# Band copies of a macaron block's FFNs on ScalarE or GpSimd

## The chip, the cores and the metric

One core of a Trainium2 chip runs the whole block. A core has five engines with a queue each, worked off in order: TensorE (PE: matmuls; PEld: its loads of weights), VectorE (DVE), ScalarE (ACT), GpSimd (POOL) and SyncE (SP, which here only issues DMAs). DMAs can also be issued from ACT's and POOL's queues. The metric is the device time of one execution in microseconds (us), as the median of several runs; lower is better.

## The reference

One layer: a gated FFN added with weight 0.5, a mixer of a short convolution and gated linear attention, a second FFN, a last norm; all in float32 on 512 rows of width 1024, hidden width 2816.

```python
def swiglu(x, w_gu, w_down):
    g, u = jnp.split(x @ w_gu, 2, axis=-1)
    return (jax.nn.silu(g) * u) @ w_down
...
    for l in range(DEPTH):
        x = x + FFN_RES_WEIGHT * swiglu(rmsnorm(x, norm_ffn1_g[l]), ffn1_w_gu[l], ffn1_w_down[l])
        x = x + hybrid_mixer(rmsnorm(x, norm_mix_g[l]), w_in[l], conv_w[l], gate_w_up[l], gate_b[l],
                             gla_norm_g[l], w_out_conv[l], w_out_gla[l], w_o[l])
        x = x + FFN_RES_WEIGHT * swiglu(rmsnorm(x, norm_ffn2_g[l]), ffn2_w_gu[l], ffn2_w_down[l])
    return rmsnorm(x, final_norm_g)
```

## The kernel before

**Products.** A float32 product is made from three matmuls in a rounded float32 type: each operand v is split into h (v cast, by ScalarE) and l = v - h (by VectorE), and h*h + h*l + l*h is summed in PSUM. For weights this is `wh` (line L386, ScalarE) and `wl` (L387, VectorE), made two steps ahead into three buffers each, from raw weights `f` that SyncE's DMAs load into ten buffers.

**Sets.** Most matrix products are cut 2 x 2 and done with seven block products instead of eight, called m1, p2, q6, p5, q7, p3 and p4 in the code. Sums of weight blocks that some of them need are made in place: by DMAs that add one `f` to another, issued from GpSimd's queue (`add`, L352), or by VectorE (L364, L394). A *tall* set turns the product round: the activations are the stationary operand and the weights the moving one of 128x512 (`Tall.run`, L712); a plain set has 128x256 (`Set.run`, L625). A tall set's seven products have two halves each, so it takes 14 steps of 12 matmuls. Some products are copied on from PSUM by ScalarE: L718 (the running sum m1), L835 and L838 (u and a kept q6), L633 (a kept q6 or q7 of a plain set).

**The hidden layer.** In an FFN's up projection, a tall set gives four of the 22 blocks of the hidden layer, but with rows and columns exchanged (tokens on partitions). The down projection needs them the other way round, in `hid`. For that VectorE turns blocks of 32 x 32 in place into `z` (L875), and then 16 copies of 32 partitions x 512 elements put each band into its place in `hid`: `move(f, a, q)` (L881) takes band a of `z`, columns of quarter q, to quarter q of `hid`'s partitions. `z` has one buffer, so the next set's turns wait for all 16 copies.

The first FFN (PLAIN1 = 4) has four tall sets (hidden blocks 4, 8, 12, 16) and then a plain one (20, 21); the copies of its last tall set are called one by one at later steps (`late_move`), down into the first steps of the down projection. The second FFN has five tall sets (0, 6, 10, 14, 18) and a plain set after the first; its last two are turned by PE (`turn`, L869), so it has 48 copies, and the first FFN 64. The other sets' 16 copies are called over the ten steps that follow the set. During the second FFN, GpSimd makes 32 copies of the same form for the residual (`natural_move`, L1060), from blocks that VectorE turns (L1054). The plain set there is turned by PE at L916.

**Order.** PE's order is as written. The other engines' order is chosen ahead of the run by a list scheduler, which knows the instructions' dependences and gives each engine one fixed queue; an instruction in `keep_in_program_order` stays behind everything written before it on its engine. Waits between engines are semaphores.

Of the kernel before, what the change touches and what calls it, by code (L numbers as in the profile page):

```python
# [234 lines left out]
def block_kernel(ctx: ExitStack, tc: tile.TileContext, xT, vecs, gf, gup, wgl, wts, out):  # L235
    nc = tc.nc
# [568 lines left out]
    def ffn(up, down, norm, nxt, plain, at):  # L805
# [71 lines left out]
        def move(f, a, q):  # L877

            src = zs[f][32 * a : 32 * (a + 1)].rearrange("p t (b r) -> p b t r", r=P)
            dst = hid[32 * q : 32 * (q + 1), f : f + 4].rearrange("p b (t r) -> p b t r", r=P)  # L880
            nc.scalar.copy(dst[:, :, :, 32 * a : 32 * (a + 1)], src[:, :, :, 32 * q : 32 * (q + 1)])  # L881

        def up_set(i):
            f = [f for kind, f in UPS[up] if kind == "set"][i]
# [122 lines left out]
        def late_move():  # L1007
            if late:
                move(*late.pop(0))
# [3 lines left out]
        for i, (kind, f) in enumerate(UPS[up]):  # L1013
            if kind == "set":
                if not plain:
                    at_step(begin(i + 1)[0], lambda f=f: turn_pair(f))
                continue
            quads = [(f, a, q) for a in range(4) for q in range(4)]
            if f in by_tensor:
                turns = (begin(i + 1) if i + 1 < len(UPS[up]) else  # L1020
                         [((down, 0), 1, "m1"), ((down, 0), 0, "p2")])
                for key, js in zip(turns, ((0, 1), (2, 3))):
                    at_step(key, lambda f=f, js=js: turn(f, js))
            elif f == last:
                late.extend(quads)
            else:
                after = keys[ends[f] + 1 : ends[f] + 11]
                for n, m in enumerate(quads):
                    at_step(after[n * len(after) // 16], lambda m=m: move(*m))
# [870 lines left out]
```

## Time and profile before

| | |
|---|---|
| median of 3 runs | 1156.43 us (1155.9 to 1156.73) |
| profiled execution | 1157.14 us, span of the trace 1155.4 us, granted TensorE clock 0.999 |
| busy share of the span | PE 99%, PEld 86%, DVE 77%, ACT 62%, POOL 13% |
| first FFN's up projection, tall sets | about 50 to 208 us |
| second FFN's tall sets with copies | about 820 to 980 us |

The profile is of one execution. Its groups read: line, engine, operation, tile written <- tiles read, shape, count | busy us, mean ns | idle us of the engine before them and what ended that idle time. In a timeline a row is start, length, engine, line, operation, tiles, count, and in brackets an idle time ahead of it with what ended it. Matmuls overlap, so their starts, not their lengths, give PE's pace.

### The profile page before, as it was taken

To read this page: it belongs to the slowest core of one execution; us is meant where nothing else is said; L and a number is where in the kernel's file an instruction comes from. 1 tells how busy PE (TensorE), PEld (TensorE's weight loads), DVE (VectorE), ACT (ScalarE), POOL (GpSimd) and SP (SyncE) were. 2 spreads that over 40 slices of the span, in tenths; PEclk is the share of its full clock that TensorE was granted. 3 is DMA by queue.
4 is the path that set the end of the run, shared out by engine and by line. 5 is a ranking of instruction groups with operands and counts; after the bars stand their busy time and mean duration, and the time that the engine had idled before them with its cause. 6 is when DMAs were issued, how large, how long until landed. Compare 5 with 4: busy or idle time off the path is not lost.

```text
span 1155.4 us, 16314 instructions
## 1 busy us (share of the span) xinstructions
PE 1144.6 (99%) x6284; PEld 996.3 (86%) x6284; DVE 893.9 (77%) x1061; ACT 714.7 (62%) x923; POOL 149.5 (13%) x191
## 2 busy tenths in 40 slices
PE   9999999999999999999999999999999999999997
PEld 7888888889988888889999998888888878888886
DVE  7976776798887975767797999555786666889966
ACT  6568778755452757565665567534668588675543
POOL 0011111001021111101011110000111344110100
PEclk9999999999999999999999999999999999999999
DMA  9587786657674386778576787934485977787711
GB/s 363 112 205 161 180 220 157 173 143 175 174 220 136 82 228 163 188 217 227 137 173 147 198 205 182 322 115 128 97 207 147 235 181 167 180 223 176 179 40 73
DMA packets 60381, 203.20 MB, mean 176 GB/s; under 512 B 6960, under 2 KB 7088, under 8 KB 60304
## 3 DMA queue, kind: packets, MB, share of 16 engines
q0 software_dynamic: 19648, 71.31, 33.6%
q1 hardware_dynamic: 38064, 126.14, 32.2%
q10 hardware_dynamic: 2592, 4.72, 1.1%
q8 instruction: 49, 0.80, 0.3%
q14 instruction: 28, 0.23, 0.1%
HBM read 124.55 MB, written 8.39 MB: 115 GB/s over the span
## 4 chain that ended last, share of the span: by engine, by line
PE 90%; ACT 6%; DVE 2%; issue 1%; ACTq 0%; POOL 0%; POOLq 0%
PE mm L712 42%; PE mm L625 24%; PE mm L443 6%; PE mm L421 3%; PE mm L419 3%; PE mm L420 3%; ACT wh L386 3%; ACT hid L881 2%; PE mm L461 1%; PE mm L460 1%; PE mm L462 1%; DVE wl L387 1%; PE mm L1161 1%; PE mm L1160 1%; PE mm L1162 1%
## 5 line engine op out<-in xcount | busy, mean ns | idle before, releaser
L387 DVE TENSOR_TENSOR wl<-f,wh 128x1024 fp32r<-128x1024 f32 (+1 forms) x349 | 424.5, 1221 | 173.2 <-ACT wh L386 168.2
L386 ACT CAST wh<-f 128x1024 fp32r<-128x1024 f32 (+1 forms) x349 | 364.3, 1048 | 297.5 <-PE mm L712 94.8
L712 PE MATMUL mm<-wh,op 128*128 128x512 f32 x1680 | 522.9, 390 | 0.0
L712 PEld LDWEIGHTS mm<-wh,op 128*128 128x128 f32 x1680 | 315.4, 188 | 65.2
L712 PE MATMUL mm<-wl,op 128*128 128x512 f32 x840 | 327.7, 390 | 1.9 <-DVE wl L387 1.8
L625 PE MATMUL mm<-op,wh 128*128 128x256 f32 x1456 | 263.4, 283 | 1.3 <-ACT tp L633 1.3
L352 POOL DMA_DIRECT2D f<-f x132 | 113.8, 865 | 895.6 <-DVE wl L387 459.1
L625 PEld LDWEIGHTS mm<-op,wh 128*128 128x128 f32 x1456 | 227.4, 192 | 2.3 <-ACT tp L633 1.5
L625 PE MATMUL mm<-op,wl 128*128 128x256 f32 x728 | 206.1, 283 | 0.1
L712 PEld LDWEIGHTS mm<-wl,op 128*128 128x128 f32 x840 | 157.7, 188 | 36.9 <-DVE wl L387 4.7
L625 PEld LDWEIGHTS mm<-op,wl 128*128 128x128 f32 x728 | 139.4, 191 | 0.3 <-DVE wl L387 0.3
L881 ACT COPY hid<-z 32x512 f32<-32x512 f32 x112 | 69.3, 618 | 5.6 <-DVE z L875 3.9
L683 ACT CAST op<-hid 128x1024 fp32r<-128x1024 f32 x42 | 44.0, 1050 | 19.6 <-PE mm L712 14.1
L684 DVE TENSOR_TENSOR op<-hid,op 128x1024 fp32r<-128x1024 f32 x42 | 51.3, 1223 | 5.2 <-ACT op L683 4.8
L421 PE MATMUL mm<-op,wl 128*128 128x512 f32 x132 | 51.5, 390 | 0.0
L420 PE MATMUL mm<-op,wh 128*128 128x512 f32 x132 | 51.4, 389 | 0.0
L419 PE MATMUL mm<-op,wh 128*128 128x512 f32 x132 | 51.4, 389 | 0.0
L443 PE MATMUL mm<-op,wh 128*128 128x512 f32 x192 | 49.0, 397 | 0.0
L443 PEld LDWEIGHTS mm<-op,wh 128*128 128x128 f32 x192 | 36.4, 192 | 8.1 <-ACT wh L386 0.4
L394 DVE TENSOR_TENSOR f<-f,f 128x1024 f32<-128x1024 f32 x26 | 31.8, 1234 | 7.1 <-issue 4.3
L421 PEld LDWEIGHTS mm<-op,wl 128*128 128x128 f32 x132 | 24.8, 188 | 5.4 <-DVE wl L387 0.3
L420 PEld LDWEIGHTS mm<-op,wh 128*128 128x128 f32 x132 | 24.8, 188 | 5.1
(331 smaller groups left out, 1197.7 us busy)
## 6 DMA issues: line engine op xcount, KB each, us to landing
f<-wts SPq DMA_DIRECT2D x219, 512.0 KB, 4.5
f<-f POOLq DMA_DIRECT2D x132, 512.0 KB, 5.2
xs<-X POOLq DMA_DIRECT2D x8, 256.0 KB, 4.1
ga<-tp ACTq DMA_DIRECT2D x8, 256.0 KB, 4.8
gb<-tp ACTq DMA_DIRECT2D x8, 256.0 KB, 5.5
tp<-ga SPq DMA_DIRECT2D x8, 256.0 KB, 6.1
tp<-gb SPq DMA_DIRECT2D x8, 256.0 KB, 5.1
X<-xs SPq DMA_DIRECT2D x8, 256.0 KB, 6.5
```

Of the source, the lines that this page charges most:

```text
L352: nc.gpsimd.dma_start(out_, a, accum_op=ALU.add)
L386: nc.scalar.copy(h[:, :w], raw[:, :w])
L387: nc.vector.tensor_tensor(out=l[:, :w], in0=raw[:, :w], in1=h[:, :w].bitcast(F32), op=ALU.subtract)
L419: nc.tensor.matmul(o, wh, ah, start=first, stop=False)
L420: nc.tensor.matmul(o, wh, al, start=False, stop=False)
L421: nc.tensor.matmul(o, wl, ah, start=False, stop=last)
L443: nc.tensor.matmul(o[c], w[:, s : s + P], a[k], start=k == 0 and j == 0, stop=k == kt - 1 and j == 2)
L625: nc.tensor.matmul(to, ww[:, s], aa[:, t], start=fresh and k == 0 and e == 0 and j == 0, stop=k == 3 and j == 2, skip_group_check=True)
L683: nc.scalar.copy(hv, v)
L684: nc.vector.tensor_tensor(out=lv, in0=v, in1=hv.bitcast(F32), op=ALU.subtract)
L712: nc.tensor.matmul(self.bank[b][e], aa[:, c], ww, start=fresh and i == 0 and n == 0, stop=k == 3 and n == 2, skip_group_check=True)
L881: nc.scalar.copy(dst[:, :, :, 32 * a : 32 * (a + 1)], src[:, :, :, 32 * q : 32 * (q + 1)])
```

## The change

In `move`, a copy whose quarter q is 1 or 3 (first FFN) or 3 (second FFN) is made by GpSimd (now at line L883) instead of ScalarE (now L885), and stays in program order there. That is 8 of the 16 copies of each of four sets in the first FFN (32), and 4 of the 16 of each of three sets in the second (12); 68 stay on ScalarE.

```diff
-            nc.scalar.copy(dst[:, :, :, 32 * a : 32 * (a + 1)], src[:, :, :, 32 * q : 32 * (q + 1)])
+            dst, src = dst[:, :, :, 32 * a : 32 * (a + 1)], src[:, :, :, 32 * q : 32 * (q + 1)]
+            if q in ((1, 3) if plain else (3,)):
+                tc.keep_in_program_order(nc.gpsimd.tensor_copy(dst, src))
+            else:
+                nc.scalar.copy(dst, src)
```

The scheduler then orders ScalarE's queue anew. Names below are the tile written and the tiles read, with their numbers. On ScalarE, in the second half of the copies of the first FFN's first tall set (z131):

```order
 L386 CAST wh152_923<-f116_706 128x1024
-L881 COPY hid20_190<-z131_794 32x16x32 x2
 L386 CAST wh154_940<-f126_753 128x1024
-L881 COPY hid20_190<-z131_794 32x16x32 x2
 L838 COPY tp156_956<-mm136_834 128x512
-L881 COPY hid20_190<-z131_794 32x16x32
 L838 COPY tp157_958<-mm137_835 128x512
 L386 CAST wh158_962<-f114_702 128x1024
-L881 COPY hid20_190<-z131_794 32x16x32 x2
 L386 CAST wh160_980<-f124_749 128x1024
-L881 COPY hid20_190<-z131_794 32x16x32
```

Ahead of wh152 stand eight copies before and eight now; ahead of wh158 and wh160 thirteen and fifteen before, and eight now. The second and third set (z180, z229) have the same pattern.

At the end of the first FFN's up projection, with the copies of its fourth tall set (z279): first ScalarE (L1067 and L683 cast operands of the down projection from `hid`, L633 empties the bank of a kept q7), then GpSimd.

```order
 L386 CAST wh295_1828<-f247_1484 128x1024
-L881 COPY hid20_190<-z279_1717 32x16x32 x3
-L1067 CAST op321_1977<-hid20_190 128x1024
+L1071 CAST op321_1977<-hid20_190 128x1024
+L885 COPY hid20_190<-z279_1717 32x16x32
+L683 CAST op325_2010<-hid20_190 128x1024
 L633 COPY tp297_1856<-mm271_1648 128x512
```

Two copies fewer and one cast more (op325) stand between wh295 and the copy out of the bank.

```order
 L352 DMA f292_1822<-f291_1820 128x1024
+L883 COPY hid20_190<-z279_1717 32x16x32
 L352 DMA f327_2014<-f329_2018 128x1024
+L883 COPY hid20_190<-z279_1717 32x16x32
 L352 DMA f328_2016<-f327_2014 128x1024
+L883 COPY hid20_190<-z279_1717 32x16x32
 L352 DMA f363_2278<-f364_2280 128x1024
```

Copies of the fourth set now stand behind adding DMAs in GpSimd's queue, the last behind the one into f328. The cast op382 on ScalarE, which reads blocks 16 to 19 of `hid`, now waits for GpSimd.

On ScalarE in the second FFN, towards the end of the copies of its second tall set (z1255; the third, z1304, is alike):

```order
 L838 COPY tp1280_8650<-mm1260_8520 128x512
-L881 COPY hid1105_7600<-z1255_8478 32x16x32
 L838 COPY tp1281_8652<-mm1261_8521 128x512
 L386 CAST wh1282_8658<-f1240_8388 128x1024
-L881 COPY hid1105_7600<-z1255_8478 32x16x32 x2
 L386 CAST wh1284_8678<-f1248_8432 128x1024
-L881 COPY hid1105_7600<-z1255_8478 32x16x32
```

Of this set's copies thirteen stood ahead of wh1282 before, and twelve do now; ahead of wh1284 fifteen before, and twelve now. In the first tall set of that FFN (z1178) the four copies between the casts wh1206 and wh1211 are gone from ScalarE.

## The prediction

> **What bounds the kernel now.** I read the engines' busy shares first, then the groups by line.
>
> ```profile
> PE 1144.6 (99%) x6284; PEld 996.3 (86%) x6284; DVE 893.9 (77%) x1061; ACT 714.7 (62%) x923; POOL 149.5 (13%) x191
> L387 DVE TENSOR_TENSOR wl<-f,wh 128x1024 fp32r<-128x1024 f32 (+1 forms) x349 | 424.5, 1221 | 173.2 <-ACT wh L386 168.2
> L881 ACT COPY hid<-z 32x512 f32<-32x512 f32 x112 | 69.3, 618 | 5.6 <-DVE z L875 3.9
> L1060 POOL COPY X<-hid 32x512 f32<-32x512 f32 x32 | 25.9, 808 | 3.7 <-DVE hid L1054 2.5
> ```
>
> TensorE (PE) is the bound: 1144.6 of 1155.4 us. ScalarE is idle for over a third of the span, so the 69.3 us of band copies cannot be worth 69.3 us; they are worth only the holes in PE that ScalarE's backlog makes. For those I followed the chain of waits through the first FFN, and looked where it leaves PE.
>
> ```profile
> 108.98 1.06 ACT wh L386
> 110.07 1.24 DVE wl L387
> 111.35 24.59 PE mm L712 x107
> ...
> 149.97 23.27 PE mm L712 x102
> ...
> 188.60 5.55 PE mm L712 x23
> ...
> 209.31 0.67 DVE z L875
> 209.98 1.12 DVE wl L387
> 211.14 2.90 PE mm L625 x22
> ...
> 220.49 0.59 ACT tp L633
> 221.12 6.01 PE mm L625 x48
> ```
>
> Rows are start, length, what. PE resumes at 111.35, 149.97 and 188.60 after a weight split (cast wh by ScalarE, remainder wl by VectorE), at 211.14 after VectorE's own burst of transposes, and at 221.12 after ScalarE emptied a PSUM bank. The chain says who came last, not how long PE stood still; that comes from PE's timeline, as the start of a matmul minus the start at which it was due.
>
> ```profile
> 187.76 0.61 PE L712 MATMUL mm<-wh,op 128*128 128x512 f32 x2
> 188.60 0.50 PE L712 MATMUL mm<-wl,op 128*128 128x512 f32 x1 [0.22 <-DVE wl L387]
> 188.94 0.40 PE L712 MATMUL mm<-wh,op 128*128 128x512 f32 x1
> ...
> 219.52 0.28 PE L625 MATMUL mm<-op,wl 128*128 128x256 f32 x1
> 221.12 0.50 PE L625 MATMUL mm<-op,wh 128*128 128x256 f32 x2 [1.32 <-ACT tp L633]
> ...
> 941.79 0.61 PE L712 MATMUL mm<-wh,op 128*128 128x512 f32 x2
> 943.12 0.50 PE L712 MATMUL mm<-wl,op 128*128 128x512 f32 x1 [0.72 <-DVE wl L387]
> ...
> 980.88 0.61 PE L712 MATMUL mm<-wh,op 128*128 128x512 f32 x2
> 981.95 0.50 PE L712 MATMUL mm<-wl,op 128*128 128x512 f32 x1 [0.45 <-DVE wl L387]
> ```
>
> The pitch of a 128x512 matmul is 24.59/107 = 0.23 us. After the two from 187.76 the next was due at 188.22 and came at 188.60: 0.38 late, and the one behind it started 0.34 instead of 0.23 later, so the hole is 0.49. The chain's rows at 111.35 and 149.97 begin the same kind of hole, which I take at the same 0.49. The 128x256 pitch is 6.01/48 = 0.125: 221.12 was due at 219.64, a hole of 1.48, about 1.58 with the restart. In the second FFN: due 942.25, came 943.12, 0.98 with the restart; due 981.34, came 981.95, 0.72. One more stands where PE turns tiles:
>
> ```profile
> 886.17 1.43 PE L916 MATMUL aux<-ident,tp 128*128 128x128 f32 x8
> 887.36 0.47 PE L712 MATMUL mm<-wh,op 128*128 128x512 f32 x1
> ...
> 1003.62 1.04 PE L869 MATMUL aux<-ident,z 128*128 128x128 f32 x8
> 1004.42 0.47 PE L712 MATMUL mm<-wh,op 128*128 128x512 f32 x1
> ```
>
> Eight turns take 1.19 from their start to the next matmul at 886.17 and 0.80 at 1003.62: 0.39 lost. All holes that ScalarE's copies can have a part in: 3 x 0.49 + 1.58 + 0.39 + 0.98 + 0.72 = 5.1 us, 0.45% of the kernel. That is the ceiling.
>
> **The change, part by part.** 32 copies of the first FFN and 12 of the second leave ScalarE's queue for GpSimd's: 44 x 0.62 = 27 us of ScalarE. What counts is how many of them stood ahead of each late instruction.
>
> Behind the first tall set of the first FFN (z131) five copies fewer stand ahead of wh158, which is the cast at 108.98 that PE waited for.
>
> ```profile
> 93.00:111.00 18.00, 18.00 (x81) 14.67 (x79) 9.33 (x9) 17.44 (x26) 2.58 (x3) 1.00 0.58 130
> ```
>
> In this stretch (columns: length, then busy us of PE, PEld, DVE, ACT, POOL) ScalarE is busy 17.44 of 18 us, so five copies fewer bring the cast 5 x 0.62 = 3.1 us forward, against 0.49 us needed: the hole goes, and PE itself is late next. Second and third set are ordered alike: 3 x 0.49 = **1.47 us**.
>
> At the hole at 221.12, behind the fourth set (z279), two copies go from ahead of L633, but the cast op325 of 1.05 us comes in: 2 x 0.62 - 1.05 = **0.19 us** of the 1.58. The rest of this hole stays, and so does the one at 211.14, which VectorE's burst makes. The second FFN:
>
> ```profile
> 881.15 2.50 ACT L881 COPY hid<-z 32x512 f32<-32x512 f32 x4
> ...
> 939.38 0.62 ACT L881 COPY hid<-z 32x512 f32<-32x512 f32 x1
> ...
> 940.50 1.05 ACT L386 CAST wh<-f 128x1024 fp32r<-128x1024 f32 x1
> ...
> 941.58 1.49 DVE L387 TENSOR_TENSOR wl<-f,wh 128x1024 fp32r<-128x1024 f32 x1 [2.21 <-ACT wh L386]
> ```
>
> At 886 the four copies from 881.15 go from ahead of the activation that the turns wait for: 2.5 us against 0.39 needed, **0.39 us**. At 943 and 982 only one copy fewer stands ahead of the late cast (12 instead of 13, the one at 939.38), 0.62 us. At 943 that leaves 0.87 - 0.62 = 0.25 and a restart if the split still takes 1.49, and nothing if it takes its usual 1.22: a gain of 0.6 to 0.98, I take **0.8**. At 982 0.61 was missing and 0.62 comes: 0.4 to 0.72, I take **0.65**.
>
> What GpSimd pays. The same copy form, 32x512, stands in its row L1060 at 808 ns mean, so 44 cost 36 us on an engine that is busy 13%. Where it pushes others:
>
> ```profile
> 895.66 5.09 POOL L1060 COPY X<-hid 32x512 f32<-32x512 f32 x6
> ...
> 900.26 1.57 DVE L387 TENSOR_TENSOR wl<-f,wh 128x1024 fp32r<-128x1024 f32 x1 [1.93 <-ACT wh L386]
> ```
>
> This split began among six copies of L1060 and took 1.57 instead of the 1.22 of L387's group: a copy in progress holds VectorE up by as much as 0.35 us, and a split holds a copy up likewise (six in 5.09 us, 0.85 each, where ScalarE takes 0.62). The bounds of this term are 0 and 44 x 0.35 = 15.4 us of VectorE. From 93 to 111 VectorE works 9.33 of 18 us and waits for casts in the rest, so there I cost it at 0: its idle time covers it, and without that cover each delay would be PE's. I charge it only at 943 and 982, in the choices above, because those two splits come with no room at all. The Trainium skill, "SBUF — State Buffer", section "Who interferes with whom", says that a VectorE instruction with two SBUF inputs contends with a GpSimd instruction that reads SBUF and that the later one fully blocks; by it a delay could reach one copy's 0.61 us, not 0.35, and at 943 and 982 nothing would be gained, 1.45 us less in the sum.
>
> GpSimd's queue also holds the DMAs that add weights (L352), and copies now stand among them. The tightest place is the end of the first FFN: the last copy of z279 stands behind the adding DMA into f328, and ScalarE's operand cast op382 gains a wait for it.
>
> ```profile
> 265.95 0.86 POOL L352 DMA_DIRECT2D f<-f  x1 [4.90 <-DVE wl L387]
> ...
> 272.94 1.04 ACT L683 CAST op<-hid 128x1024 fp32r<-128x1024 f32 x1
> ```
>
> The copy can end at 265.95 + 0.86 + 0.8 = 267.6 and is needed at 272.94: 5.3 us of room, cost 0. Earlier sets have more, since z is next written a whole set later. A DMA behind copies starts at most some copies later; six copies are 6 x 0.81 = 4.9 us, and the engine idles longer than that before most of them (L352 in the stretch from 93: 2.58 busy of 18). I cost that at 0, covered by this idle time.
>
> Sum: 1.47 + 0.19 + 0.39 + 0.8 + 0.65 = **3.5 us**. The profiled execution took 1157.14 (span 1155.4, 1.7 around it), 0.7 above the median 1156.43. Taken off: 1153.6 profiled, a span near 1151.9, and 1152.9 as the median. This measurement can tell about 0.2%, 2.3 us, from no change.
>
> **Rivals.**
> 1. Everything goes: the order at 221 turns out harmless as well, all 5.1 us: 1151.4. For it, ScalarE's other copies there shrink too; against it, the cast moved ahead of L633. 0.10.
> 2. The second FFN gives nothing, because copies in progress block the two splits that have no room: 3.5 - 1.45 = 2.05, so 1154.4. For it, the 1.49 and 1.57 us rows above; against it, only four copies per set move there. Chance 0.19. (The Trainium skill's page named above makes it the rule whenever the copy starts first; the rows here show delays of part of a copy.)
> 3. PE runs ahead and meets weights that have not landed. Nine casts already wait for loads (row below: us in total, times, longest); none of these waits reaches PE now, and one that does, at its longest, takes back 1.8 of the 3.5: 1154.7. 0.06.
>
> ```profile
> ACT wh L386 <- DMA f<-wts: 14.6, 9, 1.8
> ```
>
> Two end on the other side.
>
> 4. Slower: VectorE's splits become the bound under GpSimd's copies. 44 delays of 0.35 are 15 us; with 40% of that on PE, 6.2 us against 3.5, the kernel takes 1159. It decides from a quarter (3.5 of 15.4). Against it, VectorE idles half of these stretches. 0.04.
> 5. Slower: a copy is stuck behind an adding DMA and op382 waits. It must come 5.3 us later than worked out before it costs anything, 8.8 us later to undo the gain, and 11.4 us later for 1159. 0.03.
>
> **How the numbers follow.** My forecast has 0.58. Faster by over 0.2% (below 1154.1): forecast and rival 1, 0.68. Within 0.2%: rivals 2 and 3, 0.25. Slower: rivals 4 and 5, 0.07. The range runs from rival 1 (1151.4) to rival 3 (1154.7), each widened by the 0.5 us by which the runs shown lie from their median (1155.9 against 1156.43): 1150.9 to 1155.2. That leaves out most of rivals 4 and 5 and a little on either side.
>
> **What would show it.** The row of ScalarE's copies falls to x68, GpSimd gets x44 at 0.6 to 0.9 us. In the chain, PE runs through 111, 150 and 187 without a split before it; near 219 there is still a wait for L633 of over 1 us; the turns near 885 take 0.8; near 941 and 980 the waits for wl are below 0.3. I am wrong if PE shows new waits for wl inside the sets, if a transpose into z or an operand cast waits for GpSimd, or if the hole near 219 is gone.

## The result and the profile after

The change makes the kernel faster: 1150.49 us in the median of 6 runs (1150.15 to 1150.89) against 1156.65 for the kernel before beside it (6 runs, 1155.9 to 1157.47), a ratio of 0.9947 with an interval of 0.9934 to 0.996. That is 6.2 us, where 3.5 were forecast; the time lies 0.4 under the low end of the range. The profiled execution took 1150.53 (span 1148.8), against 1157.14 (span 1155.4).

From the page of the changed kernel, the engines' busy shares and the groups that the change touches (L883 is the new copy on GpSimd, L885 ScalarE's, L1064 the residual's copy, formerly L1060):

```profile
PE 1141.2 (99%) x6284; PEld 996.6 (87%) x6284; DVE 901.0 (78%) x1061; ACT 687.8 (60%) x879; POOL 199.1 (17%) x235
L387 DVE TENSOR_TENSOR wl<-f,wh 128x1024 fp32r<-128x1024 f32 (+1 forms) x349 | 428.0, 1231 | 164.7 <-ACT wh L386 159.7
L883 POOL COPY hid<-z 32x512 f32<-32x512 f32 x44 | 45.8, 1041 | 22.1 <-DVE z L875 20.5
L885 ACT COPY hid<-z 32x512 f32<-32x512 f32 x68 | 42.0, 618 | 2.5 <-DVE z L875 1.5
L1064 POOL COPY X<-hid 32x512 f32<-32x512 f32 x32 | 29.4, 919 | 1.5 <-DVE hid L1058 0.2
```

44 copies went over. On GpSimd one takes 1041 ns in the mean, more than the 600 to 900 forecast, and VectorE is busy 7.1 us longer (901.0 against 893.9). TensorE still sets the time: the chain of waits through the first FFN, which before came back to PE from other engines at 111.35, 149.97, 188.60, 211.14 and 221.12, now stays on it (start, length, what):

```profile
85.96 105.63 PE mm L712 x466
191.58 2.87 PE mm L625 x24
194.46 10.91 PE mm L712 x48
205.36 17.27 PE mm L625 x144
```

PE's holes, measured as before (start of a matmul minus the start at which it was due, restarts included), in us:

| place in the kernel before | before | after |
|---|---|---|
| 111, 150, 188 (splits behind the tall sets) | 3 x 0.49 | 0 |
| 211 (split of a plain step) | 0.36 | 0 |
| 221 (wait for L633) | 1.58 | 0 |
| 886 (turns) | 0.39 | 0.09 |
| 943 | 0.98 | 0.30 |
| 982 | 0.72 | 0 |

Together 5.1 us less. PE runs its 6284 matmuls in one order in all kernels, so their starts can also be compared one by one. By that count the change ends 6.6 us earlier: 0.9 in the first 25 us, ahead of any tall set's copies; 3.7 between 100 and 230; 2.0 from 880 on; nothing elsewhere. So 5.7 us lie behind the copies, and the table has all but small delays beside its places (0.12 near 228, 0.13 near 893, and 0.04 to 0.06 at each of the three splits).

PE's timeline after, at the last two places where something is left: the eight turns now take 0.80 from their start to the next matmul, and one wait for a split remains.

```profile
881.56 1.03 PE L920 MATMUL aux<-ident,tp 128*128 128x128 f32 x8
882.36 0.48 PE L712 MATMUL mm<-wh,op 128*128 128x512 f32 x1
```

```profile
936.63 0.61 PE L712 MATMUL mm<-wh,op 128*128 128x512 f32 x2
937.27 0.50 PE L712 MATMUL mm<-wl,op 128*128 128x512 f32 x1
```

### The profile page after: what moved, and what is told of

The parts are those of the page before. It is cut to its first block, busy times and chain, and to the rows that moved or that the text cites. A ratio compares the mean times of both kernels' runs of the same rounds, so it can differ in the third digit from the quotient of the medians.

```text
span 1148.8 us, 16324 instructions
## 1 busy us (share of the span) xinstructions
PE 1141.2 (99%) x6284; PEld 996.6 (87%) x6284; DVE 901.0 (78%) x1061; ACT 687.8 (60%) x879; POOL 199.1 (17%) x235
## 4 chain that ended last, share of the span: by engine, by line
PE 98%; DVE 1%; ACT 1%; issue 0%; ACTq 0%; POOL 0%; POOLq 0%
PE mm L712 49%; PE mm L625 25%; PE mm L443 6%; PE mm L420 3%; PE mm L419 3%; PE mm L421 3%; PE mm L461 1%; PE mm L460 1%; PE mm L462 1%; PE mm L1166 1%; PE mm L1164 1%; PE mm L1165 1%; PE aux L1510 1%; PE aux L1513 0%; PE aux L1493 0%; PE aux L281 0%
## 5 line engine op out<-in xcount | busy, mean ns | idle before, releaser
L625 PEld LDWEIGHTS mm<-op,wh 128*128 128x128 f32 x1456 | 227.4, 192 | 0.7
L625 PEld LDWEIGHTS mm<-op,wl 128*128 128x128 f32 x728 | 139.4, 192 | 0.0
L683 ACT CAST op<-hid 128x1024 fp32r<-128x1024 f32 x42 | 44.0, 1050 | 22.5 <-PE mm L712 14.1
L883 POOL COPY hid<-z 32x512 f32<-32x512 f32 x44 | 45.8, 1041 | 22.1 <-DVE z L875 20.5
L885 ACT COPY hid<-z 32x512 f32<-32x512 f32 x68 | 42.0, 618 | 2.5 <-DVE z L875 1.5
L443 PEld LDWEIGHTS mm<-op,wh 128*128 128x128 f32 x192 | 36.2, 190 | 7.6
L394 DVE TENSOR_TENSOR f<-f,f 128x1024 f32<-128x1024 f32 x26 | 34.5, 1342 | 5.0 <-issue 3.9
L1064 POOL COPY X<-hid 32x512 f32<-32x512 f32 x32 | 29.4, 919 | 1.5 <-DVE hid L1058 0.2
```

The lines of the kernel that those rows point to most:

```text
L443: nc.tensor.matmul(o[c], w[:, s : s + P], a[k], start=k == 0 and j == 0, stop=k == kt - 1 and j == 2)
L625: nc.tensor.matmul(to, ww[:, s], aa[:, t], start=fresh and k == 0 and e == 0 and j == 0, stop=k == 3 and j == 2, skip_group_check=True)
L683: nc.scalar.copy(hv, v)
L883: tc.keep_in_program_order(nc.gpsimd.tensor_copy(dst, src))
```

## Where the holes at 211 and 221 came from

The prediction gave the hole at 221 a gain of 0.19 and the one at 211 none, and both went wholly. It put the one at 211 down to VectorE's transposes. But the chain of waits before, a few rows further up than the prediction showed it, leads from these transposes back to the cast at 205.25, and from there on to L633 as well:

```profile
205.25 1.06 ACT wh L386
206.34 1.23 DVE wl L387
207.56 1.20 DVE tp L594 x2
...
214.04 0.60 DVE z L875
215.29 0.62 ACT hid L881
```

What changed ahead of that cast is seen on VectorE, GpSimd and ScalarE. Before (rows: start, length, engine, line, operation, tiles, count, idle time ahead and what ended it by the profile):

```profile
188.58 1.23 DVE L364 TENSOR_TENSOR f<-f,f 128x1024 f32<-128x1024 f32 x1
...
190.33 0.86 POOL L352 DMA_DIRECT2D f<-f  x1 [11.25 <-ACT hid L881]
197.22 0.86 POOL L352 DMA_DIRECT2D f<-f  x1 [6.03 <-DVE wl L387]
...
205.25 1.05 ACT L386 CAST wh<-f 128x1024 fp32r<-128x1024 f32 x1 [4.39 <-PE mm L712]
...
220.49 0.58 ACT L633 COPY tp<-mm 128x512 f32<-128x512 f32 x1
```

And after:

```profile
183.84 1.22 DVE L364 TENSOR_TENSOR f<-f,f 128x1024 f32<-128x1024 f32 x1 [0.30 <-DMA f<-wts]
...
186.74 0.86 POOL L352 DMA_DIRECT2D f<-f  x1 [6.15 <-DVE wl L387]
192.95 0.86 POOL L352 DMA_DIRECT2D f<-f  x1 [5.35 <-DVE tp L840]
...
200.05 1.06 ACT L386 CAST wh<-f 128x1024 fp32r<-128x1024 f32 x1 [1.75 <-DMA f<-f]
...
215.10 0.58 ACT L633 COPY tp<-mm 128x512 f32<-128x512 f32 x1
```

The same five steps stand 3.6 to 5.4 us earlier, while PE itself is 2.6 ahead there. The third set's copies (z229) on ScalarE had made the cast at 186.23 late; behind its remainder on VectorE the sum at L364 was late; GpSimd's first adding DMA overwrites a block that this sum reads, so it waits for the sum, and the second for the first to land; and the cast of wh280 reads what the second wrote. The times of the semaphores in the traces bear out each link. Before, the sum ended at 189.80, and the first add started 0.53 later; it landed at 196.71, and the second started 0.51 later; that landed at 205.15, and the cast started 0.10 later. After, the sum ended at 185.06, and what the first add waited for was a load of weights, which landed at 186.18. So copies of one set cost PE time 35 us later, behind the next set, by way of two transfers.

The lateness at GpSimd is not all of it. Against PE, the cast came 2.6 us earlier: 1.0 is the earlier first add, and 1.6 is that the two transfers took 5.7 and 7.0 us from start to landing, where they took 6.4 and 7.9 before. In the twelve traces they take 5.4 to 7.0 and 5.6 to 8.2. What sets their time, no run shows.

The profile of before named PE as what ended the cast's idle time of 4.39 us, and I believed it; the profile of after names the transfer. (The names in the adds' rows, ACT hid and DVE wl, mislead in the same way.) The row of such a DMA does not show its landing: 0.86 us long at 192.95, while the data landed at 199.95 and the cast behind it starts at 200.05. The Trainium skill, "Perfetto Trace Analysis", section "DMA Instruction — SWDGE (GPSIMD)", says as much: the interval shown ends with the last descriptor, not with the data.

## The experiments

Each stood beside the kernel before on the same chip: 1156.38 us in the first group, 1156.52 in the second, 1156.55 in the third. Unless said otherwise, the edit is to the changed kernel's one line of condition, `if q in ((1, 3) if plain else (3,)):`, and nothing else.

**One FFN alone.**

```diff
+            if plain and q in (1, 3):
```

> Only the first FFN's 32 copies go to GpSimd. My theory: the holes near 111, 150, 187, 211 and 221 us all go (3 x 0.49 + 0.37 + 1.58 = 3.4 us against the kernel before, about 1153.2), and those near 886, 943 and 982 stay at 0.4, 1.0 and 0.7. Rival (the prediction's own account, and something else in the second FFN for the rest): 1.7 us, about 1155, with a hole of over 1 us near 219.

1153.1 us, ratio 0.9973 (0.9961 to 0.9984): 3.3 us of gain. The holes at 111, 150, 188 and 211 are gone and the second FFN's are there, but 0.5 is left of the one at 221, which the theory had go. In the first FFN the queues hold the change's order; the first add started 0.9 us earlier than there, but the two took 6.8 and 8.0 us to land instead of 5.7 and 7.0. So a part of this hole comes and goes with the time of the transfers.

```diff
+            if not plain and q == 3:
```

> Only the second FFN's copies with q == 3 go to GpSimd (12 of 48); the first FFN's all stay on ScalarE. Theory (the gain is the sum of the holes that the chain of late casts made): the holes near 886, 943 and 982 lose 0.39, 0.68 and 0.73 us as in the whole change, 1.8 us together, so 1154.6 against 1156.4; the first FFN's holes (111, 150, 188, 211, 221) stay at 0.49, 0.49, 0.49, 0.4 and 1.6. Rival (the second FFN gives more than its holes show, by what the whole change and the first FFN alone differ, 1153.1 - 1150.5 = 2.6 us): 1153.8. Second rival (of the prediction: the second FFN's turns are paced by something other than the copies): 1156.2 or more.

1154.58 us, ratio 0.9981 (0.9972 to 0.999): 1.9 us, which is the theory's 1.8. The first FFN's holes are all there. The two parts alone, 3.3 and 1.9, add up to 5.2, near the 5.1 of the table; as each is known to 1.0 to 1.3 us, that is agreement in size and no more.

**One set alone, and all but that one.** The first FFN's sets write `hid` from block f = 4, 8, 12, 16; the condition is narrowed to f == 12 (third set), f == 16 (fourth), and to all but f == 12 (no set of the second FFN starts there).

```diff
+            if plain and f == 12 and q in (1, 3):
```

> Only eight copies of the first FFN's third tall set go to GpSimd. Theory: the backlog of this set makes not only the hole at 188 but, by way of the sum f262 and the two adding DMAs into f246 and f244 behind it, the late transposes of the fourth set, and so the holes at 211 and 221: 0.49 + 0.37 + 1.58 = 2.4 us gained, about 1154.2, with holes left only near 111, 150 and in the second FFN. Rival: the hole at 221 belongs to the fourth set's own copies ahead of the bank's evacuation; then 0.5 us is gained, about 1156.1, and 211 and 221 stay.

```diff
+            if plain and f == 16 and q in (1, 3):
```

> Only eight copies of the first FFN's fourth tall set go to GpSimd. Theory: its own copies are not what makes the hole at 221; 0.2 us gained (two copies fewer, one cast more ahead of the evacuation), about 1156.4, hole still 1.3 or more. Rival: 1.6 us gained, about 1155.0, hole gone.

```diff
+            if f != 12 and q in ((1, 3) if plain else (3,)):
```

> The change without the third set: its 16 copies stay on ScalarE. Theory: the holes at 188, 211 and most of 221 come back, 0.49 + 0.37 + 1.4 = 2.3 us slower than the whole change, about 1152.8. Rival: only 0.5 us is given back, about 1151.0.

The third set alone: 1154.32 us, ratio 0.9983 (0.9974 to 0.9992), 2.1 us of gain. PE's holes at 188, 211 and 221 are gone, 111 and 150 stay. The fourth alone: 1156.38, ratio 1.0 (0.9991 to 1.0009), and all holes stay, 1.27 us at 219 and 0.58 at 211, which is 0.31 less and 0.22 more than before. So what stands between wh295 and L633, which the prediction had counted copy by copy, is worth 0.3 us at that hole and nothing that shows in the time. All but the third: 1152.28, ratio 0.9966 (0.9953 to 0.9978), 1.8 us above the change. The holes of 0.49 at 186 and of 1.12 near 217 are back; the one at 211 isn't, though the theory had it come back too. The first add starts 1.7 us behind the hole at 186 and takes 6.4 to land, both as before; the second took 7.4 instead of 7.9, about what is missing at 211 and 221. ScalarE and GpSimd there:

```profile
188.38 0.86 POOL L352 DMA_DIRECT2D f<-f  x1 [11.25 <-ACT hid L885]
195.28 0.86 POOL L352 DMA_DIRECT2D f<-f  x1 [6.04 <-DVE wl L387]
...
202.74 1.05 ACT L386 CAST wh<-f 128x1024 fp32r<-128x1024 f32 x1 [3.87 <-DMA f<-f]
...
217.67 0.58 ACT L633 COPY tp<-mm 128x512 f32<-128x512 f32 x1
```

One caution on single profiles: with the first FFN, the third or the fourth set alone, the second FFN shows 0.5 to 0.8 us more of holes than before, though its queues hold the order of before. By so much two executions can differ there.

**Without the second add.** A direct test of the link: the kernel before, ScalarE making all 112 copies, with one adding DMA left out, the one at 197.22 (the 26th of `add`; a part of the sum of weights is then missing).

```diff
-        def add(self, out_, a):
-            nc.gpsimd.dma_start(out_, a, accum_op=ALU.add)
+        def add(self, out_, a, nth=iter(range(999))):
+            if next(nth) not in (25,): nc.gpsimd.dma_start(out_, a, accum_op=ALU.add)
```

> The kernel before, with all copies on ScalarE, but without the one weight add into f244 that GpSimd issued at 197.22 us (this leaves a part of the weights' sum out of the computation). Theory (the hole at 221 follows the landing of that add at 205.15, through the cast of wh280 right behind it): the cast starts when its buffer is free, near 201 to 203, the wait for L633 near 220 shrinks from 1.58 us to under 0.3, the hole of 0.4 near 211 goes as well, and the time is 1154.4 to 1155.0 against 1156.5, though ScalarE still makes all of its copies. Rival (the reading on record: the cast is paced by PE, and the fourth set's copies on ScalarE make L633 late): the hole stays at 1.4 us or more and the time at 1156.2 or more.

1154.32 us, ratio 0.9982 (0.9974 to 0.9991): 2.2 us. Its adds, the cast, the copy out of the bank, and then the chain of waits behind the third set:

```profile
189.75 0.86 POOL L352 DMA_DIRECT2D f<-f  x1 [11.23 <-ACT hid L881]
204.51 0.86 POOL L352 DMA_DIRECT2D f<-f  x1 [13.90 <-DVE wl L387]
```

```profile
201.90 1.06 ACT L386 CAST wh<-f 128x1024 fp32r<-128x1024 f32 x1 [1.67 <-PE mm L712]
...
217.35 0.58 ACT L633 COPY tp<-mm 128x512 f32<-128x512 f32 x1
```

```profile
188.01 5.51 PE mm L712 x23
193.52 2.87 PE mm L625 x24
196.40 10.91 PE mm L712 x48
207.30 17.27 PE mm L625 x144
```

The cast now does wait for PE, 1.67 us and no more; PE runs from 188.01 through both places without a hole, while 111, 150 and 188 are as they were. The other instructions stand in the order of before on every queue. So both holes hang on this one transfer, and ScalarE's copies of the fourth set, all still there, do no harm. Put beside each other, with PE's need taken as 0.12 us behind the start of its matmul before:

| kernel | first add | second add | cast of wh280 | L633 starts | PE wants its result | hole |
|---|---|---|---|---|---|---|
| before | 190.33 | 197.22 | 205.25 | 220.49 | 219.6 | 1.58 |
| all but the third set | 188.38 | 195.28 | 202.74 | 217.67 | 217.3 | 1.12 |
| copies twice (below) | 187.30 | 194.81 | 201.89 | 216.83 | 217.1 | 0.48 |
| the change | 186.74 | 192.95 | 200.05 | 215.10 | 216.7 | 0 |
| without the second add | 189.75 | none | 201.90 | 217.35 | 218.7 | 0 |

From the cast to L633 it takes 14.9 to 15.5 us in all five, and L633 another 0.6. The hole is what remains.

**What GpSimd can bear.** All copies on GpSimd, then each of the 44 made twice.

```diff
+            if True:
```

> All 112 copies of the tall sets go to GpSimd. Theory (VectorE and GpSimd hold each other up and GpSimd's queue is in order): a copy there took 1.04 us in the mean against 0.62 on ScalarE, so a set's 16 take some 17 us of GpSimd against 10 of ScalarE before; the weight adds queue behind them and the last copies come some 5 us later than in the change, against 1.6 us that the wait for L633 near 215 has to spare. So the gain is lost again in part or whole: 1152 to 1160, with holes of 1 us and more behind every set. Rival (only what ScalarE is rid of counts, GpSimd's time is free): at or under the change, 1149.5 to 1150.5.

1154.83 us (11 runs, 1152.63 to 1156.42), ratio 0.9982 (0.9973 to 0.9991): faster than before by 1.7 and slower than the change by 4.3, so the theory's size came and the rival's didn't. But its place was wrong. In the profiled execution, the fastest of the 11, the first FFN has no holes at all, with GpSimd busy 31.7 of the 55 us from 170 to 225; the largest hole is in the second FFN. There the residual's copies use the same queue, the adds come late behind them, and four casts in a row and a sum (L394) wait for transfers (the last of them and the sum below), where in the change the casts at this place wait for PE:

```profile
958.67 4.35 POOL L883 COPY hid<-z 32x512 f32<-32x512 f32 x4
...
963.45 1.05 ACT L386 CAST wh<-f 128x1024 fp32r<-128x1024 f32 x1 [1.45 <-DMA f<-f]
...
963.43 1.32 DVE L394 TENSOR_TENSOR f<-f,f 128x1024 f32<-128x1024 f32 x1 [0.87 <-DMA f<-f]
...
965.94 0.50 PE L712 MATMUL mm<-wl,op 128*128 128x512 f32 x1 [1.71 <-DVE wl L387]
```

What makes the slower ten runs up to 3.8 us slower than this one, no trace shows.

```diff
+                for _ in range(2):
+                    tc.keep_in_program_order(nc.gpsimd.tensor_copy(dst, src))
```

> As the change, but every copy on GpSimd is made twice in a row (the same values to the same place), so that GpSimd and its lock on the memory beside VectorE are used twice as long and ScalarE's part is unchanged. Theory (the copies on GpSimd lie beside other work; VectorE has spare time of 20 per cent): a set's GpSimd part rises from 8.3 to 16.6 us (first FFN); an add may come some us later, but most lands ahead of its cast: 1150.5 to 1152. Rival (GpSimd's time is near the path, the change just fits): each set comes 3 to 8 us later than its splits are wanted, 1155 or more.

1153.2 us (1151.52 to 1154.19), ratio 0.9969 (0.9957 to 0.998): 2.7 us slower than the change, between the two expectations. Two of the places are adding DMAs again: the second add at 194.81 instead of 192.95 (0.48 us of hole, in the table), and at 251 a hole of 1.6 us. The add ahead of that one starts at 243.28, where the change has 239.10. Of these 4.2 us, 1.7 are the two copies ahead of it, which took 4.17 beside VectorE's two-input operations, where the change has one of 2.44. The other 2.4, of which PE's own lateness is 0.9, are that the add before waited so much longer for a sum of VectorE (L364), which here works without a pause from 215.83 on, with three operations stretched to 1.6 us by the doubled copies:

```profile
239.15 4.17 POOL L884 COPY hid<-z 32x512 f32<-32x512 f32 x2
243.28 0.86 POOL L352 DMA_DIRECT2D f<-f  x1
```

```profile
247.92 1.05 ACT L386 CAST wh<-f 128x1024 fp32r<-128x1024 f32 x1 [7.06 <-DMA f<-f]
```

**Half in both FFNs.**

```diff
+            if q in (1, 3):
```

> Half of the copies in both FFNs go to GpSimd (24 of 48 in the second in place of 12). Theory: what is left of ScalarE's lateness in the second FFN is the hole of 0.30 us near 937 and 0.1 near 882; with half of the copies gone the cast ahead of 937 comes 1.2 us earlier, and the time is 1150.0 to 1150.4. Rival (GpSimd's queue, which there also has the 32 copies of L1064 and the adds, is the bound): the 12 copies more cost 12 x 1.04 = 12.5 us of GpSimd over three sets, the adds come up to 4 us later and a hole of 1 us or more opens: 1151.5 to 1154.

1150.43 us (1150.24 to 1150.55), ratio 0.9946 (0.9933 to 0.9958). The 0.30 at 937 is gone, the span is 1148.2 instead of 1148.8, and the change repeated in the third group has 1150.63: a difference of 0.1 to 0.2 us, which these runs do not tell from none. No hole over 0.1 us is left at any of these places, so this is as far as moving the copies goes.

**The change again.**

> The whole change, unaltered, beside the kernel before on the chip of this call. The holes that went come to 5.3 us and the medians of the first comparison differ by 6.2. Theory (the holes are all of it): 5.3 us under the kernel before, 1151.2 at 1156.5. Rival (half a microsecond or more comes from elsewhere): 6.0 us or more under it.

1150.63 us (1150.16 to 1151.35), ratio 0.995 (0.9936 to 0.9964), 5.9 us under the kernel before. It falls between theory and rival, and the interval (4.2 to 7.4 us) holds both. The profiles say more. Matmul by matmul, this execution gains 5.6 us behind the first copies, and the one of the first comparison 5.7. The other 1.2 and 0.9 of the spans' differences lie in the first 25 us, where no edit changes the order of a queue and the profile of the kernel before is the slowest of the twelve (the others are 0.3 to 1.3 ahead of it). So that part is a difference between executions. What the medians, 6.2 and 5.9, show beyond 5.7 is well within their intervals.

## The prediction, step by step

- **Three holes of 0.49 (1.47).** Right: all three are gone, and the splits are out of the chain. That such a hole belongs to its own set is shown for the third, which alone removed just the one at 188 of the three; the first and second set were only moved together.
- **Hole at 221 (0.19), hole at 211 (0).** This is the step that failed, and that the hole near 219 is gone is the sign of being wrong that I had named. I counted the instructions between wh295 and L633, where the change does little (fourth set alone: 0.3 at this hole, 0 in the time), and took the cast at 205.25 as paced by PE because its row said so. It waited for an adding DMA, which the third set's copies had delayed. The term was worth 1.58 and 0.36 instead of 0.19, some 1.75 us, most of the 2.2 that my 3.5 lacked of the 5.7.
- **The ceiling of 5.1** was too low: the hole at 211, which I charged to VectorE's burst, belonged in it too, and 5.7 came.
- **Turns at 886 (0.39), 943 (0.8), 982 (0.65).** 0.30, 0.68 and 0.72: a sum of 1.7 against 1.84. Rival 2 (nothing from the second FFN) is out: that part alone gained 1.9. The hole left at 937 is where the lock below takes its share, as I had allowed in the choice of 0.8.
- **GpSimd's and VectorE's cost (0).** Right on PE's path, though the size was missed: 1041 ns for a copy instead of 808. VectorE's 7.1 us over 44 copies are 0.16 us for each, under half of the bound of 0.35, though a single operation was stretched by up to 0.41: 23 of the 44 copies took their usual 0.60 to 0.62. Rival 4, VectorE's splits as the bound, did not come. With twice the copies (14.1 us more on VectorE, 908.0) late adds made 2.1 of the 2.7 us lost, and VectorE's lateness had a part in one of them. Rival 5 did not come either.
- **Rival 3 (weights not landed).** The casts wait for loads less than before: 6.7 us in four waits, where 14.6 in nine stood.

```profile
ACT wh L386 <- DMA f<-wts: 6.7, 4, 1.8
```

- **Chances.** Rival 1, that everything goes, is what happened, at 0.10. I worked it out as harmless order at 221; its cause was a link that I had not looked for.

## What to carry to other kernels

A hole that stands far behind a busy engine's backlog may still be made by it: follow each late instruction through every step that it waits for, the transfers issued from another engine's queue above all, until the chain reaches work that is early, and do not stop at the engine which the row names. Count a queue's relief by the deadline it feeds and not by its busy time: 27 us taken off ScalarE gave 5 to 6, and the same copies made twice on GpSimd cost nearly half of that again, by way of the adds behind them and of VectorE's work beside them.

## What was unexpected in the hardware

GpSimd is no slower than ScalarE at this copy if left alone: 0.61 us against 0.62. With a two-input VectorE operation on the way, the one that comes second waits almost until the other has ended. Both sides stand in this piece of the changed kernel, GpSimd's copies and then VectorE's operations:

```profile
92.35 2.99 POOL L883 COPY hid<-z 32x512 f32<-32x512 f32 x2 [2.54 <-DVE z L875]
```

```profile
92.13 1.18 DVE L387 TENSOR_TENSOR wl<-f,wh 128x1024 fp32r<-128x1024 f32 x1
93.23 3.18 DVE L394 TENSOR_TENSOR f<-f,f 128x1024 f32<-128x1024 f32 x2
```

Two copies take 2.99 us, 1.5 each, and the two sums L394 take 3.18, 1.6 each where 1.22 is usual. Over the trace 23 of the 44 copies took 0.60 to 0.62 us and 18 took 1.43 to 1.62; one that met two such operations took 2.44. A VectorE operation is stretched by up to 0.41. That is much nearer to exclusion in turn, which the Trainium skill states in "SBUF — State Buffer", section "Who interferes with whom", than to the shared pace that I had read from the 0.85 of L1060, which came of four copies of 0.61, one of 0.94 and one of 1.51; the price on VectorE's side stays under the length of a copy.
